# Latent x in four transfers with 16 grid columns outermost, and the first up-projection weights split during the output projection

## The chip, the cores and the metric

The kernel runs on one core of a Trainium2 chip, as one program. Its time is the device time of that core in microseconds (us), as the median of several runs. A profile of one execution goes with it. TensorE is called PE in the profile, ScalarE ACT, VectorE DVE, GpSimd POOL and SyncE SP; SyncE issues nearly all DMA transfers of this kernel.

## The reference

One layer of a hybrid diffusion backbone on two sets of tokens: 128 context tokens and 512 latent tokens, the latter on a grid of 8 rows and 64 columns, with 1024 channels each. All is float32. Both pass the same layer with their own modulation:

```python
def _layer(x, cond, attend, ...):
    sa, ca, ga, sf, cf, gf = _modulation(cond, w_mod, b_mod)
    h = _modulated_norm(x, norm_mix_g, sa, ca)
    p, q, k, v, gp, gn = _mixer_inputs(h, w_in, q_norm_g, k_norm_g)
    na = attend(q, k, v)
    pool = _pool_mixer(p, pool_w, pool_scale)
    x = x + ga * _merge(pool, na, gp, gn, w_pool_proj, w_na_proj, w_o)
    h = _modulated_norm(x, norm_ffn_g, sf, cf)
    x = x + gf * _conv_ffn(h, w_up, ffn_conv_w, ffn_conv_b, w_down)
    return x, k, v
```

`_modulated_norm` is an RMS norm over the channels, times (1 + scale), plus shift. Context tokens attend to each other. A latent token attends to the 128 cached keys and to a neighbourhood of 8 rows and 16 columns, with a bias for each head and relative position; the kernel takes queries in four blocks of 16 grid columns, each against a band of 32 columns. Pooling (windows of 2 to 16 tokens) and the width-3 convolution run along the token sequence in grid order, that is row after row.

## The kernel before

Every float32 product is made of three matmuls on a high and a low part: a weight tile `raw` is loaded by `load_raw`, and `split_to` makes `whi` (a cast on ScalarE, line 133) and `wlo` (a subtraction on VectorE, line 134). `load_w` does both. Tokens lie in five tiles of 128: tile 0 is the context, tiles 1 to 4 hold 16 grid columns of all 8 rows each, as two half-blocks of 8 columns (`hb`), each of them row after row.

The start, lines 302 to 337, is the stage that the first half of the change touches. The order of SyncE's issues is fixed: the small `vec`, two tiles `wm` of modulation weights, the context x (`in_xc`), latent tiles 1 and 2 into `vv`, the first value weights `wtok`, latent tiles 3 and 4 into `na` (both are borrowed memory), then further pairs `wm` and tiles `wtok` as the six buffers of `sp` come free. `load_x` issues two transfers a latent tile, one for each half-block, from `xl_blocks`, whose dimensions are half-block, row, column, channel. `normalise(t)` squares the tile on ScalarE (line 275), takes the root (277), scales on VectorE (280), transposes on TensorE (284) and copies the result to `xnT` (288, 290). `make_h` then makes `hhi` and `hlo`. `mod_rows` multiplies a pair `wm` with the conditioning on TensorE (149), and `tok_step` makes the value product (203 to 205), eight steps over the channels, in turn with those. Each DMA of SyncE marks its landing with one of eight semaphores taken in turn, and a later DMA with the same one waits for the earlier.

`to_grid_order` brings a result for all tokens from the order of the half-blocks into grid order; `blocks` is the view that it reads, `grid` the view that it writes. It is used in `gate_steps` for 16 gates (line 440, through `tanh_half`) and in `pool_group` for four pooling groups (434 to 437). `att_values` multiplies the attention's result by the inverse sums and writes it in grid order, 16 times for latent blocks (550). The bias table is laid out on the host by `_layout` in the same token order.

Later, the output projection runs in two halves of 512 channels: the first with `tok_step`, the second token tile by token tile in `out_product`, with the second norm's `second_h` in between. Then `up_a`, `up_w` and `up_b` make the up-projection. The first block's weights, `ra` and `rg`, are loaded and split behind that loop in the code, by lines 894 to 899. The order in which the engines get their instructions is not that of the code alone: a scheduler with a timeline of its own sets it when the program is built.

Of the kernel before, what the change touches and what calls it, by code (L numbers as in the profile page):

```python
# [11 lines left out]
F32R = mybir.dt.float32r  # L12
# [5 lines left out]
P = 128  # L18
# [6 lines left out]
ROWS = 8  # L25
# [3 lines left out]
NF = DFF // P  # L29
# [35 lines left out]
def body(ctx, tc, A):  # L65
    nc = tc.nc
    MULT, ADD, SUB, MIN = ALU.mult, ALU.add, ALU.subtract, ALU.min
# [6 lines left out]
    def pool(stack, name, bufs=1, side="left", space=bass.MemoryType.SB):  # L74
        return stack.enter_context(tc.tile_pool(name=name, bufs=bufs, space=space, reuse_waits="tile",
                                                side=side if space == bass.MemoryType.SB else None))
# [5 lines left out]
    wp = pool(ctx, "wp")  # L82
# [33 lines left out]
    def ps_small():  # L116
        return PS.tile([P, 512], F32, tag="sm", name="sm", bufs=8 - NACC)
# [6 lines left out]
    def load_raw(src, tp=None):  # L124
        r = (tp or wp).tile([P, 1024], F32, tag="raw", name="raw", bufs=SRAW if tp else 3)
        dma = nc.sync.dma_start(r, src)
        if tp or pinned[0] > 0:
            tc.keep_in_program_order(dma)
            pinned[0] -= 0 if tp else 1
        return r  # L130

    def split_to(raw, hi, lo):
        nc.scalar.copy(hi, raw)  # L133
        nc.vector.tensor_tensor(out=lo, in0=raw, in1=hi.bitcast(F32), op=SUB)  # L134
# [111 lines left out]
    xts = [VV[:, 2 * t:2 * t + 2, :].rearrange("p a b -> p (a b)") for t in range(3)]  # L246
    nas = na.rearrange("p a b -> p (a b)")
    xts += [nas[:, t * D:(t + 1) * D] for t in range(2)]

    xl_blocks = A["xl"].rearrange("(r hb c) d -> hb r c d", r=ROWS, c=8)  # L250
    junk = hlo.rearrange("p a b -> p (a b)")

    def load_x(t):
        if t == 0:
            nc.sync.dma_start(xts[0], A["xc"])
        else:
            for hb in range(2):
                nc.sync.dma_start(xts[t][hb * 64:hb * 64 + 64, :], xl_blocks[2 * (t - 1) + hb])

    def load_wv():  # L260
        wr.append(load_raw(A["wtok"][len(wr)], sp))
# [42 lines left out]
    for t in range(3):  # L304
        load_x(t)
    rows[0] = mod_scale_shift(0, rows[0])
    load_wv()
    for t in range(3, 5):
        load_x(t)
# [29 lines left out]
    for t in range(5):  # L339
        dst = VX if t == 0 else V[t - 1]  # L340
# [86 lines left out]
        return ap.rearrange("p (r hb c) -> p hb r c", r=ROWS, c=8)  # L427

    def blocks(ap):
        return ap.rearrange("p (hb r c) -> p hb r c", r=ROWS, c=8)  # L430

    def to_grid_order(fn, ctx_dst, lat_dst, ps):

        fn(ctx_dst, ps[0][:, :SEQ])
        d = grid(lat_dst)
        fn(d[:, 0:3], blocks(ps[0][:, SEQ:320]))
        fn(d[:, 3:8], blocks(ps[1][:, :320]))
# [97 lines left out]
    def att_values(pair, n, pts, rb):  # L535
        cs = CHUNKS[n]
        o = ps_small()
        for i, vt in enumerate(cs):
            for h in range(2):
                hd = (2 * pair + h) * DH  # L540
                nc.tensor.matmul(o[h * DH:(h + 1) * DH, :P], lhsT=vt[:, hd:hd + DH], rhs=pts[h][:, i * P:(i + 1) * P],  # L541
                                 start=(i == 0), stop=(i == len(cs) - 1))
        nc.tensor.transpose(o[:, P:2 * P], rb.rearrange("p a b -> p (a b)"), ident)
        r = at.tile([P, P], F32, name="rt", bufs=2)
        nc.scalar.copy(r, o[:, P:2 * P])
        if n == 4:
            nc.vector.tensor_tensor(out=na[:, pair, 0:SEQ], in0=o[:, :P], in1=r, op=MULT)
        else:
            dst = na[:, pair, SEQ:].rearrange("p (r n hb c) -> p n hb r c", r=ROWS, n=4, hb=2)[:, n]
            nc.vector.tensor_tensor(out=dst, in0=o[:, :P].rearrange("p (hb r c) -> p hb r c", hb=2, r=ROWS),  # L550
                                    in1=r.rearrange("p (hb r c) -> p hb r c", hb=2, r=ROWS), op=MULT)

    units = [(p, n) for p in range(4) for n in (4, 0, 1, 2, 3)]
    probs, pts = {}, {}
    for i in range(len(units) + 2):
        if i < len(units):
            probs[i] = att_scores(*units[i])
        next(mods, None)
        gate_fill(GF[0])
        if i - 1 in probs:  # L560
            pts[i - 1] = att_transpose(units[i - 1][1], *probs.pop(i - 1))
        gate_fill(GF[1])
        if i - 2 in pts:
            att_values(*units[i - 2], *pts.pop(i - 2))
        next(mods, None)
# [68 lines left out]
    for g in range(4):  # L634
        d = pool_group(g)
# [88 lines left out]
    for u in range(4):  # L724
        r = load_raw(A["wo"][4 + u])
# [76 lines left out]
    TI = {(4, HB): 0, (0, 0): 4, (0, HB): 8, (4, 0): 12}  # L802
    J = ((0, 64), (64, 192), (192, HB))

    xns = []
    for t in range(5):
        xns.append(out_product(t, lambda t: second_h(t, xns[t])))
# [8 lines left out]
    fw = pool(e6, "fw", 1, "right")  # L816
# [22 lines left out]
    def halves_of(w):  # L839
        return [tuple(x[:, i * 512:(i + 1) * 512] for x in w) for i in range(2)]  # L840
# [50 lines left out]
        nc.scalar.copy(ug[:, h1], pa[:, cs])  # L891


    ra, rg = load_raw(A["wup"][0]), load_raw(A["wup"][NF])
    w0 = []
    for tp_, r, e in ((wp, ra, ""), (fw, rg, "2")):
        hi, lo = [tp_.tile([P, 1024], F32R, tag=x + e, name=x + e, bufs=1 if e else 2) for x in ("whi", "wlo")]
        split_to(r, hi, lo)
        w0.append(halves_of((hi, lo)))

    def plain(x1_, x2_, n, c0):
        for (wa, wb), u in zip(w0, (us["a"][0], us["g"][0])):
# [133 lines left out]
def _layout(inp):  # L1036
# [30 lines left out]
    p, q, k, v, gp, gn = np.split(wi, np.cumsum([512, 512, 512, 512, 1024]), axis=1)  # L1067
# [14 lines left out]
    for g, w in enumerate(WINDOWS):  # L1082
        for c0, n in ((0, SEQ), (SEQ, LAT)):
            t = np.arange(n)
# [6 lines left out]
    r, c = np.arange(ROWS), np.arange(8)  # L1091
    idx = np.empty((4, P, 256), np.int64)
    for n in range(4):
        kb = min(max(16 * n - 8, 0), 32)
        qr = np.broadcast_to(r[None, :, None], (2, 8, 8)).reshape(-1)
        qc = (16 * n + 8 * np.arange(2)[:, None, None] + 0 * r[None, :, None] + c[None, None, :]).reshape(-1)
        kr = np.broadcast_to(r[None, :, None], (4, 8, 8)).reshape(-1)
        kc = (kb + 8 * np.arange(4)[:, None, None] + 0 * r[None, :, None] + c[None, None, :]).reshape(-1)
        ws = np.clip(qc - WIN_W // 2, 0, GRID_W - WIN_W)[:, None]
        ok = (kc[None] >= ws) & (kc[None] < ws + WIN_W)  # L1100
        dr = kr[None] - qr[:, None] + 7
        dc = np.clip(kc[None] - qc[:, None] + 15, 0, 30)
        idx[n] = np.where(ok, dr * 31 + dc, 15 * 31)
# [27 lines left out]
```

## Time and profile before

| what | us |
|---|---|
| median of 3 runs | 928.6 |
| lowest, highest | 926.58, 931.41 |
| profiled execution | 925.25 |
| its span, first to last instruction | 923.5 |
| TensorE busy in it | 873.9 (95%) |
| VectorE busy | 680.4 (74%) |
| ScalarE busy | 397.0 (43%) |
| GpSimd busy | 280.3 (30%) |

The profiled execution's own time is 1.75 us more than its span, for what lies around the first and the last instruction. The busy share is a mean over stages with different limits; where time can be won is read from the chain of work that ended last and from single stretches. "Releaser" is what ended an engine's idle time.

### The profile page before, as it was taken

Reading aid. Unit: us, or ns where it says so; the run is one execution under the profiler, and the core shown is the slowest. Engines: PE = TensorE matmul, PEld = TensorE weight load, DVE = VectorE, ACT = ScalarE, POOL = GpSimd, SP = SyncE. Lnnn points to the kernel's source line nnn. Section 1 sums busy time; section 2 is a strip of 40 time slices with the busy share of each in tenths; the row PEclk is TensorE's granted clock in tenths of the full one; section 3 lists DMA queues with packets and bytes.
Section 4 is the critical chain, followed back from the end, with each engine's and each line's share of the span. In section 5 each row is a group of like instructions: output and inputs, shape, how many; then the busy total and the mean of one; then the engine's idle time right before and its main releaser. Section 6 shows DMA issues by size and latency. Waiting matters only on the chain.

```text
span 923.5 us, 13399 instructions
## 1 busy us (share of the span) xinstructions
PE 873.9 (95%) x5234; PEld 783.5 (85%) x5234; DVE 680.4 (74%) x998; ACT 397.0 (43%) x712; POOL 280.3 (30%) x206
## 2 busy tenths in 40 slices
PE   3799999999998999999889899999999999999688
PEld 2578898887898999988689799999999999898677
DVE  3456986897479633535699888879788797887696
ACT  4351344445443422225766453635435354453340
POOL 2122000000000021322206434444334543339956
PEclk9999999999999999999989999999999999999989
DMA  8758425664365222264222421213222141222213
GB/s 235 248 206 270 153 75 171 200 227 137 104 197 159 73 84 73 70 233 155 92 69 103 137 78 59 92 61 122 70 69 92 46 136 51 89 92 80 92 45 115
DMA packets 33024, 112.20 MB, mean 121 GB/s; under 512 B 3857, under 2 KB 4529, under 8 KB 32705
## 3 DMA queue, kind: packets, MB, share of 16 engines
q1 hardware_dynamic: 31840, 107.91, 35.5%
q0 software_dynamic: 1120, 3.44, 1.3%
q8 instruction: 41, 0.67, 0.3%
q14 instruction: 23, 0.18, 0.1%
HBM read 104.50 MB, written 5.78 MB: 119 GB/s over the span
## 4 chain that ended last, share of the span: by engine, by line
PE 75%; DMA 8%; DVE 8%; POOL 4%; issue 3%; ACT 2%; SPq 0%; DVEq 0%; ACTq 0%; POOLq 0%
PE acc L836 22%; PE acc L219 20%; PE sm L989 4%; PE sm L990 4%; PE sm L991 4%; PE acc L203 3%; PE acc L205 3%; PE acc L204 3%; DVE wlo L134 2%; DMA na<-in_xl 2%; POOL acc L953 2%; DMA raw<-in_wo 2%; DVE cv L926 1%; DMA raw<-in_wup 1%; PE sm L541 1%
## 5 line engine op out<-in xcount | busy, mean ns | idle before, releaser
L133 ACT CAST whi<-raw 128x1024 fp32r<-128x1024 f32 (+1 forms) x86 | 81.2, 946 | 192.3 <-PE acc L836 73.6
L134 DVE TENSOR_TENSOR wlo<-raw,whi 128x1024 fp32r<-128x1024 f32 (+1 forms) x86 | 104.4, 1215 | 39.7 <-ACT whi L133 38.8
L836 PE MATMUL acc<-th,whi 128*128 128x322 f32 (+1 forms) x336 | 104.8, 316 | 7.0 <-ACT whi L133 4.3
L836 PE MATMUL acc<-th,wlo 128*128 128x322 f32 (+1 forms) x336 | 105.6, 315 | 1.3 <-DVE wlo L134 1.3
L836 PE MATMUL acc<-tl,whi 128*128 128x322 f32 (+1 forms) x336 | 105.4, 314 | 0.0
L219 PE MATMUL acc<-hhi,whi 128*128 128x320 f32 x320 | 91.7, 320 | 0.4 <-ACT t L440 0.4
L219 PE MATMUL acc<-hlo,whi 128*128 128x320 f32 x320 | 89.5, 313 | 0.0
L219 PE MATMUL acc<-hhi,wlo 128*128 128x320 f32 x320 | 88.6, 313 | 0.0
L858 POOL TENSOR_TENSOR ws<-raw 128x512 f32<-128x512 f32 x21 | 30.2, 1438 | 168.8 <-DVE wlo L134 104.3
L989 PE MATMUL sm<-dhi,ahi 128*128 128x512 f32 x190 | 72.6, 397 | 3.6 <-ACT dhi L133 1.7
L990 PE MATMUL sm<-dlo,ahi 128*128 128x512 f32 x190 | 75.1, 395 | 0.0
L836 PEld LDWEIGHTS acc<-th,whi 128*128 128x128 f32 x336 | 63.9, 191 | 10.3 <-ACT whi L133 5.8
L991 PE MATMUL sm<-dhi,alo 128*128 128x512 f32 x190 | 72.4, 395 | 0.0
L836 PEld LDWEIGHTS acc<-th,wlo 128*128 128x128 f32 x336 | 64.4, 192 | 3.1 <-DVE wlo L134 1.8
L836 PEld LDWEIGHTS acc<-tl,whi 128*128 128x128 f32 x336 | 64.3, 191 | 1.5
L133 ACT CAST whi<-ws 128x1024 fp32r<-128x1024 f32 x42 | 43.2, 1046 | 51.3 <-PE acc L836 41.0
L134 DVE TENSOR_TENSOR wlo<-ws,whi 128x1024 fp32r<-128x1024 f32 x42 | 53.6, 1292 | 13.3 <-ACT whi L133 13.3
L1001 DVE TENSOR_TENSOR acc<-sm,acc 128x512 f32<-128x512 f32 (+1 forms) x85 | 55.8, 676 | 9.2 <-PE sm L991 9.0
L836 PE MATMUL acc<-b1l,whi 128*128 128x322 f32 x184 | 57.8, 316 | 3.8 <-DVE b1l L134 3.8
L219 PEld LDWEIGHTS acc<-hhi,whi 128*128 128x128 f32 x320 | 58.2, 191 | 2.8 <-issue 1.3
L219 PEld LDWEIGHTS acc<-hlo,whi 128*128 128x128 f32 x320 | 58.2, 191 | 0.8 <-issue 0.7
L836 PE MATMUL acc<-b1h,whi 128*128 128x322 f32 x184 | 57.5, 316 | 0.8 <-ACT b1h L133 0.8
(322 smaller groups left out, 2313.6 us busy)
## 6 DMA issues: line engine op xcount, KB each, us to landing
raw<-in_wup SPq DMA_DIRECT2D x44, 512.0 KB, 4.6
mw<-in_wmT SPq DMA_DIRECT2D x32, 512.0 KB, 4.6
raw<-in_wdn SPq DMA_DIRECT2D x22, 512.0 KB, 3.4
raw<-in_wmt SPq DMA_DIRECT2D x20, 512.0 KB, 3.5
raw<-in_wm SPq DMA_DIRECT2D x16, 512.0 KB, 9.3
raw<-in_wtok SPq DMA_DIRECT2D x12, 512.0 KB, 11.6
bias<-in_bias SPq DMA_DIRECT2D x16, 384.0 KB, 4.7
raw<-in_wab SPq DMA_DIRECT2D x8, 512.0 KB
```

The costliest lines, as they stand in the source:

```text
L133: nc.scalar.copy(hi, raw)
L134: nc.vector.tensor_tensor(out=lo, in0=raw, in1=hi.bitcast(F32), op=SUB)
L203: nc.tensor.matmul(ps[t], lhsT=xh, rhs=wh, start=(kt == 0), stop=False)
L204: nc.tensor.matmul(ps[t], lhsT=xh, rhs=wl, start=False, stop=False)
L205: nc.tensor.matmul(ps[t], lhsT=xl, rhs=wh, start=False, stop=(kt == KT - 1))
L219: nc.tensor.matmul(o[:, :n], lhsT=w[:, k], rhs=cut(x, k, c, n), start=st and a, stop=sp and b)
L836: upped[0] = nc.tensor.matmul(ps[:, cs], lhsT=a[:, c], rhs=b[:, k, cs], start=start and first, stop=last, skip_group_check=skip and not st ...
L858: nc.gpsimd.tensor_tensor(out=s[:, 1], in0=a21, in1=a22, op=ADD)
L989: nc.tensor.matmul(ps, lhsT=xh, rhs=hi[:, sl], start=(j == 0), stop=False)
L990: nc.tensor.matmul(ps, lhsT=xh, rhs=lo[:, sl], start=False, stop=False)
L991: nc.tensor.matmul(ps, lhsT=xl, rhs=hi[:, sl], start=False, stop=(j == GRP - 1))
L1001: nc.vector.tensor_tensor(out=o, in0=ps, in1=o, op=ADD)
```

## The change

Latent x comes in one transfer a tile, four in all, with the 16 columns of the tile as the outermost dimension, then the 8 rows. Inside a half-block the tokens so stand column after column and no longer row after row; `blocks`, the multiplication of `att_values` and the host's bias indices follow. And the first block's up-projection weights are loaded ahead of the loop over `out_product`, one of the two split there.

```diff
-    xl_blocks = A["xl"].rearrange("(r hb c) d -> hb r c d", r=ROWS, c=8)
+    xl_blocks = A["xl"].rearrange("(r t c) d -> t c r d", r=ROWS, c=16)
...
         else:
-            for hb in range(2):
-                nc.sync.dma_start(xts[t][hb * 64:hb * 64 + 64, :], xl_blocks[2 * (t - 1) + hb])
+            nc.sync.dma_start(xts[t], xl_blocks[t - 1])
...
     def blocks(ap):
-        return ap.rearrange("p (hb r c) -> p hb r c", r=ROWS, c=8)
+        return ap.rearrange("p (hb c r) -> p hb r c", r=ROWS, c=8)
...
-            nc.vector.tensor_tensor(out=dst, in0=o[:, :P].rearrange("p (hb r c) -> p hb r c", hb=2, r=ROWS),
-                                    in1=r.rearrange("p (hb r c) -> p hb r c", hb=2, r=ROWS), op=MULT)
+            nc.vector.tensor_tensor(out=dst, in0=blocks(o[:, :P]), in1=blocks(r), op=MULT)
...
+    w0a, rg = load_w(A["wup"][0]), load_raw(A["wup"][NF])
     xns = []
     for t in range(5):
         xns.append(out_product(t, lambda t: second_h(t, xns[t])))
...
-    ra, rg = load_raw(A["wup"][0]), load_raw(A["wup"][NF])
-    w0 = []
-    for tp_, r, e in ((wp, ra, ""), (fw, rg, "2")):
-        hi, lo = [tp_.tile([P, 1024], F32R, tag=x + e, name=x + e, bufs=1 if e else 2) for x in ("whi", "wlo")]
-        split_to(r, hi, lo)
-        w0.append(halves_of((hi, lo)))
+    hi, lo = [fw.tile([P, 1024], F32R, tag=x, name=x, bufs=1) for x in ("whi2", "wlo2")]
+    split_to(rg, hi, lo)
+    w0 = [halves_of(w0a), halves_of((hi, lo))]
```

In `_layout` the four index lines of the bias (queries `qr`, `qc`, keys `kr`, `kc`) swap the places of row and column in the same way.

What the built program makes of it on SyncE, at its first transfers: before, from the context x on, with the semaphores that each waits for:

```order
L255 DMA vv<-in_xc 128x1024
L258 DMA vv<-in_xl 64x1x1024 x4
L126 DMA raw<-in_wtok 128x1024 [waits DMAHW0_49]
L258 DMA na<-in_xl 64x1x1024 [waits DMAHW1_49]
L258 DMA na<-in_xl 64x1x1024 [waits DMAHW2_49]
L258 DMA na<-in_xl 64x1x1024 [waits DMAHW3_49]
L258 DMA na<-in_xl 64x1x1024 [waits DMAHW4_49]
L126 DMA raw<-in_wm 128x1024 [waits DMAHW5_49]
L126 DMA raw<-in_wm 128x1024 [waits DMAHW6_49]
L126 DMA raw<-in_wm 128x1024 [waits DMAHW7_49]
```

And with the change, the same place, to the same second pair of `wm`:

```order
L256 DMA vv<-in_xc 128x1024
L258 DMA vv<-in_xl 128x1x1024 x2
L126 DMA raw<-in_wtok 128x1024
L258 DMA na<-in_xl 128x1x1024
L258 DMA na<-in_xl 128x1x1024 [waits DMAHW0_49]
L126 DMA raw<-in_wm 128x1024 [waits DMAHW1_49]
L126 DMA raw<-in_wm 128x1024 [waits DMAHW2_49]
L126 DMA raw<-in_wm 128x1024 [waits DMAHW3_49]
```

Half of the x transfers are gone, and with them most of the waits ahead of the second `wm` pair: the eight semaphores go round later, so that the last x transfer waits for the first one (`vec`), where before the fifth to eighth waited for the `wm` pair, the context x and the first half of latent tile 1.

On ScalarE, at the output projection: the last `mhi`, the casts of that projection's weights (`whi` and `w1h`), the first two casts for the up-projection (the last `whi` row), and the squares of the residual. Before:

```order
L133 CAST whi<-raw 128x1024
L666 ACTIVATE mhi<-t_613 128x640
L133 CAST w1h<-raw 128x1024
L133 CAST whi<-raw 128x1024 x2
L133 CAST w1h<-raw 128x1024 x3
L133 CAST whi<-raw 128x1024 x2
L717 ACTIVATE o_t,sq_4051<-x_4042 128x512 x5
```

With the change:

```order
L133 CAST whi<-raw 128x1024
L665 ACTIVATE mhi<-t_609 128x640
L133 CAST w1h<-raw 128x1024
L133 CAST whi<-raw 128x1024 x2
L133 CAST w1h<-raw 128x1024 x3
L133 CAST whi<-raw 128x1024 x2
L716 ACTIVATE o_t,sq_4047<-x_4038 128x512 x5
```

Nothing moved here but the numbers of lines and buffers: the up-projection's first cast stood ahead of the squares already. The same holds for the other engines: TensorE, VectorE, ScalarE and GpSimd run the same rows in the same order before and after.

## Rows read from the trace of the kernel before

**Rows 1.** The page of the whole span: the chain that ended last.

```profile
PE 75%; DMA 8%; DVE 8%; POOL 4%; issue 3%; ACT 2%; SPq 0%; DVEq 0%; ACTq 0%; POOLq 0%
PE acc L836 22%; PE acc L219 20%; PE sm L989 4%; PE sm L990 4%; PE sm L991 4%; PE acc L203 3%; PE acc L205 3%; PE acc L204 3%; DVE wlo L134 2%; DMA na<-in_xl 2%; POOL acc L953 2%; DMA raw<-in_wo 2%; DVE cv L926 1%; DMA raw<-in_wup 1%; PE sm L541 1%
```

**Rows 2.** The chain in order of time, 0 to 80: start, us, what.

```profile
2.60 9.11 DMA vv<-in_xl
...
11.72 16.92 DMA na<-in_xl
...
31.62 1.57 PE sm L284 x8
33.19 1.86 PE sm L149 x16
```

**Rows 3.** Windows: length, busy time by engine, granted clock, DMA share, GB/s.

```profile
0.00:8.00 8.00, 1.95 (x16) 0.43 (x16) 0.50 (x3) 3.29 (x6) 1.99 (x9) 1.00 0.76 254
6.00:8.00 2.00, 1.27 (x12) 0.20 (x8) 0.00 (x0) 0.00 (x0) 0.00 (x0) 1.00 1.03 393
9.84:28.72 18.88, 8.65 (x31) 6.82 (x32) 8.10 (x16) 7.76 (x16) 2.84 (x2) 1.00 0.90 224
12.00:14.00 2.00, 1.55 (x8) 1.57 (x8) 0.30 (x1) 0.59 (x1) 0.00 (x0) 1.00 0.51 164
14.00:20.00 6.00, 2.35 (x10) 1.57 (x8) 2.08 (x6) 3.14 (x8) 0.00 (x0) 1.00 0.95 253
24.00:26.00 2.00, 0.08 (x1) 0.09 (x1) 0.10 (x1) 2.00 (x5) 0.00 (x0) 1.00 1.05 199
32.00:36.00 4.00, 4.00 (x26) 2.09 (x25) 2.00 (x6) 1.56 (x4) 0.00 (x0) 0.57 0.52 177
36.00:72.00 36.00, 36.00 (x237) 26.68 (x236) 20.51 (x39) 15.32 (x22) 7.17 (x3) 1.00 0.64 224
```

**Rows 4.** DMA issues of the whole span: operation, count, KB each, us to landing.

```profile
raw<-in_wm SPq DMA_DIRECT2D x16, 512.0 KB, 9.3
...
vv<-in_xl SPq DMA_DIRECT2D x4, 256.0 KB
na<-in_xl SPq DMA_DIRECT2D x4, 256.0 KB
...
vv<-in_xc SPq DMA_DIRECT2D x1, 512.0 KB
...
vv<-in_cv POOLq DMA_DIRECT2D x1, 256.0 KB, 6.8
...
vec<-in_vec SPq DMA_DIRECT2D x1, 131.0 KB, 2.1
```

**Rows 5.** SyncE's issues in order of time, 0 to 40: start, us.

```profile
2.60 2.71 SPq L258 DMA_DIRECT2D vv<-in_xl  x4
...
5.83 6.48 SPq L258 DMA_DIRECT2D na<-in_xl  x4
13.34 6.44 SPq L126 DMA_DIRECT2D raw<-in_wm  x4
```

**Rows 6.** ScalarE in order of time: the first and the last Square of x.

```profile
9.84 1.06 ACT L275 ACTIVATE hlo<-vv 128x1024 fp32r<-128x1024 f32 x1 [1.19 <-DMA vv<-in_xc]
...
28.72 1.06 ACT L275 ACTIVATE hlo<-na 128x1024 fp32r<-128x1024 f32 x1 [2.66 <-DMA na<-in_xl]
```

**Rows 7.** Groups by shape, whole span: busy us, mean ns, idle before.

```profile
L440 ACT ACTIVATE t<-acc 128x320 f32<-128x320 f32 x16 | 7.0, 440 | 0.0
...
L550 DVE TENSOR_TENSOR na<-sm,rt 128x128 f32<-128x128 f32 x16 | 4.5, 282 | 0.9 <-ACT rt L545 0.9
...
L440 ACT ACTIVATE t<-acc 128x128 f32<-128x128 f32 x16 | 4.4, 274 | 0.0
```

**Rows 8.** Waits of TensorE, 120 to 400: us in total, times, longest.

```profile
PE acc L219 <- ACT t L440: 0.4, 1, 0.4
```

**Rows 9.** ScalarE in order of time, 416 to 430: first up-projection cast.

```profile
423.17 1.05 ACT L133 CAST whi<-raw 128x1024 fp32r<-128x1024 f32 x1 [2.38 <-DMA raw<-in_wup]
```

More of the change, by code (lines that the diff above doesn't have):

```diff
@@ L1094, in _layout @@
         kb = min(max(16 * n - 8, 0), 32)
[L1095 to L1098, printed above, removed]
+        qr = np.broadcast_to(r[None, None, :], (2, 8, 8)).reshape(-1)
+        qc = (16 * n + 8 * np.arange(2)[:, None, None] + c[None, :, None] + 0 * r[None, None, :]).reshape(-1)
+        kr = np.broadcast_to(r[None, None, :], (4, 8, 8)).reshape(-1)
+        kc = (kb + 8 * np.arange(4)[:, None, None] + c[None, :, None] + 0 * r[None, None, :]).reshape(-1)
         ws = np.clip(qc - WIN_W // 2, 0, GRID_W - WIN_W)[:, None]
```

## The prediction

> **What bounds the kernel now.** I read the chain that ended last first, because only time on it can be won. Over the whole span 75% of it is TensorE and 8% are DMAs, and one item of that 8% stands out by name: the transfers of the latent x into the tiles na, 2% [rows 1]. The chain in order of time shows where they lie: from 2.60 to 28.64 us it consists of x transfers alone, 9.11 us into the tiles vv and 16.92 into na; then come the last tile's transposes at 31.62 and, at 33.19, the product with the second pair of modulation weights, after which the chain stays on TensorE [rows 2]. From 36 to 72 us TensorE is busy 36.00 of 36.00 us while the DMA engines are busy 0.64 of the time [rows 3]. So the start waits for x, and what follows is a train of matmuls that is not starved: if it leaves earlier, everything behind it moves.
>
> Why x is slow is in the windows. Its eight transfers are of 256 KB and go to 64 partitions each, beside transfers of 512 KB to 128 [rows 4]. At 12 to 14 us the DMA share is 0.51 at 164 GB/s, against 1.03 and 393 GB/s at 6 to 8 us [rows 3]: about half of the 16 DMA engines work. The outermost dimension of an x transfer's source is 8 (grid rows); that a transfer is dealt out over as many engines as this count is my inference from the half share. At 32 to 36 us the share is again 0.52, when x has long landed, which I read as the same eight engines working off the weights that queued behind x. SyncE is held up too: the four issues into na take 6.48 us and the next four 6.44, where the four into vv take 2.71 [rows 5].
>
> **The change part by part.** *The x loads.* Eight transfers become four of twice the size, with the same bytes, on 128 partitions and with an outermost count of 16. The order of SyncE's instructions shows the issues: before, each of the last four x transfers waits for an earlier transfer's semaphore (there are eight, taken in turn); after, only the very last waits, for the small vec load of the start. So x is issued by about 6 us, and the weights behind it follow sooner.
>
> When has the last x tile landed? Ahead of it and with it stand vec (131 KB), two modulation tiles and one value-weight tile, the context x and four x tiles (eight of 512 KB), and the cached values (256 KB) [rows 4]: 4483 KB, 4.59 MB. By 8 us 254 GB/s x 8 us = 2.03 MB have gone [rows 3], so 2.56 MB are left. From the bytes to the consumer's start there is a lag: the context x ends at 131 + 3 x 512 + 256 KB = 1.97 MB, that is at about 8 us, and its Square starts at 9.84 [rows 6]: 1.8 us. The rate isn't known, because no row shows this pattern. Its upper end is 393 GB/s (all engines on contiguous loads): 6.5 us, data at 16.3. The lower is 199 GB/s at 24 to 26 us, when the engines were as busy (1.05) but slow, with x among the traffic: 12.9 us, data at 22.7. Nearest are the same rows on half the engines, 164 x 2 = 328, and x mixed with weights as it will be, 253 at 14 to 20 us [rows 3]. I take the middle, 290: 2.56 / 0.290 = 8.8 us, data at 8 + 8.8 + 1.8 = 18.6.
>
> The last tile's Square starts at 28.72 now [rows 6]. It can't come before the work ahead of it: between 9.84 and 28.72 ScalarE is busy 7.76 us and VectorE 8.10 [rows 3], so not before 9.84 + 8.10 = 17.9 even with no wait between them. ScalarE's order is unchanged: the Square of tile 4 stands behind the root of tile 3, and that behind a cast that waits for VectorE, so some waiting stays. I take 19.7, 1.8 after that bound and 1.1 after the data. Gain 28.72 - 19.7 = 9.0 us; at the fast end 28.72 - 17.9 = 10.8; with data at 22.7 it is 6.0.
>
> What is late next? The pair of modulation weights right behind x in the queue: 1024 KB, 1.05 MB more, 3.61 in all. TensorE reads them at 33.19, 4.5 us after that Square [rows 2, 6], so they are needed at 24.2. At 290 GB/s they are there at 8 + 12.4 + 1.8 = 22.2, in time; at 199 at 27.9, and the gain is then 33.19 - 27.9 = 5.3. Behind that the loads come as buffers fall free, as before, and the share of 0.64 leaves room. TensorE's clock is the other uncertainty: the granted clock is 0.57 of full from 32 to 36 us, right behind the wait for x [rows 3]. The new start will have such a stretch too; 3 us more or less of half clock are 1.5 us either way.
>
> *The order inside a half-block.* Tokens now stand by column, then row, so blocks() reads PSUM and the tile rt in steps of 8 elements where it read straight on. It concerns 16 gates and 4 pooling groups on ScalarE and 16 multiplications on VectorE. I cost them at nothing: a straight read with a stepped write (320 elements, 440 ns) is no dearer than the straight copy next to it, 274 ns for 128, with 0.86 ns for each element more [rows 7]; no row shows a stepped read. What hides a little more is TensorE's lead over ScalarE: it waited for these gates once, 0.4 us [rows 8]. The other end of the bound is that every such element takes twice its time: 512 x 0.86 = 0.44 us, 20 times 8.8, and 16 x 0.28 = 4.5 on VectorE [rows 7]; 13.3 us if all of it lay on the path.
>
> [...]
>
> *The up-projection weights.* In the order of the built program nothing moves: the cast of these weights stands behind the output projection's own casts before and after, and it already runs at 423.17, during that projection [rows 9]. The split of the second tile is left where it was. So 0 us: nothing is moved that would need a cover, and there is no gain either.
>
> **Sum.** The profiled execution takes 925.25 us for its span of 923.5. Forecast 925.25 - 9.0 = 916.2. The median of the runs shown is 928.6, 3.35 above the profiled one, and the prediction is for such a median: 928.6 - 9.0 = 919.6.
>
> **The rivals.** *x stays slow* (same side, smaller). The rows of x that one engine fetches are still 256 KB apart in memory. For it: at 24 to 26 us a share of 1.05 brought only 199 GB/s, so something other than the number of engines is slow while x is fetched. Against: 253 GB/s at 14 to 20 us with the same rows in flight. Gain 5.3, or 923.3; at 170 GB/s, little above what half the engines gave, the weights are there at 31.0 and the gain is 2.2, or 926.4.
>
> [...]
>
> *Hidden anyway* (no change). The weight pair becomes the last arrival. For it: it stands behind x in the same queue, and TensorE waits for it next. Against: at 290 GB/s it is 2 us early, and to eat the whole gain it would have to come at 33.19, a rate of 3.61 / 23.4 = 154 GB/s, less than even half the engines gave. Time 926 to 929.
>
> *Stepped reads* (the other side). The gates and the multiplications take longer, and TensorE waits at the accumulators for them. It decides from 9.0 us of loss on; the 13.3 bounded above leave 4.3 over, a time of 932.9 at the most. Against: all of it would have to lie on the path, where one wait of 0.4 us shows now.
>
> *The change does nothing.* For the weights this is my forecast; for x the built program does show four transfers to 128 partitions.
>
> **How the numbers follow.** Half a percent, 4.6 us, is about what a measurement of this kernel can tell from no change: the three runs lie 4.8 apart. Forecast, gain 7 to 10: 0.60. More, up to the 10.8 of the fast end and the clock's 1.5: 0.08. x stays slow, gain 2 to 7: 0.20, two thirds of it above 4.6. Hidden: 0.07. Stepped reads: 0.05, of which 0.03 slower by more than 0.5% where other losses join. That makes faster 0.60 + 0.08 + 0.13 = 0.81, slower 0.03, and the same 0.16. The range goes from the fast end with the clock's 1.5 us and the spread of a median of such runs, 0.8, 928.6 - 13.1 = 915.5, to the lower part of the slow rival, a gain of 2.6: 926.
>
> **What would show it.** The last Square on x at 19 to 20.5 us in place of 28.72; SyncE's four x issues done by 6 us; a DMA share near 1 until about 22 us with no stretch at 0.5; the second weight pair's product at about 24 and the same full TensorE behind it; the gates still at 440 ns and the multiplications at 282; the casts of the up-projection weights 9 us earlier, like all their neighbours. If the Square comes at 20 and the span falls by less than 5, the train was starved later; if the first 20 us stay under 200 GB/s, x stayed slow.

## The result, and the profile after

The median is 918.94 us (four runs, 917.25 to 920.83); the kernel before, timed in turn with it on the same chip, has 927.59 (four runs, 926.05 to 931.41). The ratio is 0.9894, 95% interval 0.9869 to 0.992: faster, by 8.65 us, where 9.0 were forecast. The profiled execution took 920.83 us, its span is 919.1.

The chain that ended last, from the page of the changed kernel, answers to [rows 1] (line numbers have moved by one or two in places: L836 is L837 now, L989 to L991 are L987 to L989):

```profile
PE 77%; DVE 8%; POOL 4%; DMA 4%; issue 3%; ACT 2%; SPq 0%; DVEq 0%; ACTq 0%; POOLq 0%
```

DMA has gone from 8% to 4%. The same chain in order of time, 0 to 80 us (start, us, what), answers to [rows 2]:

```profile
4.83 14.42 DMA na<-in_xl
19.27 1.15 ACT hlo L275 x2
20.41 0.47 ACT xnT L290
20.89 0.31 ACT hhi L299
21.24 1.22 PE acc L203 x2
...
24.17 1.92 PE sm L284 x16
26.09 1.00 PE sm L149 x16
27.09 0.43 PE acc L203
```

Of x transfers 14.42 us are left where [rows 2] have 9.11 and 16.92. They end at 19.27 in place of 28.72, and behind them stands no transfer, only ScalarE and TensorE at work: the last tile's transposes and the product with the second pair of modulation weights (26.09 in place of 33.19) follow one another. The tile is another one, too: the chain of before ended x with the fourth latent tile, this one with the third, whose Square is the one at 19.27.

The windows of the changed kernel, columns as in [rows 3]:

```profile
0.00:8.00 8.00, 1.82 (x16) 0.43 (x16) 0.50 (x3) 3.29 (x6) 1.99 (x9) 1.00 0.73 250
6.00:8.00 2.00, 1.44 (x16) 0.20 (x8) 0.00 (x0) 0.00 (x0) 0.00 (x0) 1.00 1.02 401
12.00:14.00 2.00, 0.77 (x4) 0.80 (x5) 1.00 (x3) 1.54 (x4) 0.00 (x0) 1.00 1.05 248
14.00:20.00 6.00, 4.89 (x22) 3.91 (x20) 5.17 (x8) 3.60 (x6) 2.11 (x1) 1.00 1.04 245
22.00:24.00 2.00, 2.00 (x7) 1.42 (x6) 1.21 (x3) 1.24 (x4) 0.00 (x0) 1.00 1.01 401
32.00:36.00 4.00, 4.00 (x23) 2.68 (x23) 3.17 (x5) 0.94 (x3) 2.39 (x1) 1.00 0.84 314
36.00:72.00 36.00, 36.00 (x212) 27.84 (x211) 21.12 (x38) 13.36 (x19) 9.47 (x11) 1.00 0.67 229
```

No stretch stands at half a share any more: the 0.51 at 12 to 14 us is 1.05. But while x is in flight all sixteen engines bring only about 245 GB/s, and 401 before and behind it. TensorE is full from 36 to 72 us as before.

SyncE's issues in order of time (start, us) answer to [rows 5], and ScalarE's squares (start, us, idle time before in brackets) to [rows 6]:

```profile
2.60 1.36 SPq L258 DMA_DIRECT2D vv<-in_xl  x2
...
4.83 1.24 SPq L258 DMA_DIRECT2D na<-in_xl  x2
6.11 6.68 SPq L126 DMA_DIRECT2D raw<-in_wm  x4
```

```profile
10.63 1.06 ACT L275 ACTIVATE hlo<-vv 128x1024 fp32r<-128x1024 f32 x1 [1.85 <-DMA vv<-in_xc]
...
19.27 1.06 ACT L275 ACTIVATE hlo<-na 128x1024 fp32r<-128x1024 f32 x1 [1.46 <-DMA na<-in_xl]
...
21.42 1.06 ACT L275 ACTIVATE hlo<-na 128x1024 fp32r<-128x1024 f32 x1
```

The last Square stands at 21.42, 7.3 us earlier, and shows no idle time in front of it. Two things end there together: ScalarE's work ahead of it (the copy at 20.32, a cast, the root from 21.09 to 21.38) and the landing of the fourth latent tile, issued at 5.41 and there 16.0 us later, at 21.40. The issues at work between 6 and 7.5 us (KB each, us to landing; the two of `wm` are the second pair, landed at 22.4 and 23.7):

```profile
raw<-in_wm SPq DMA_DIRECT2D x2, 512.0 KB, 16.4
na<-in_xl SPq DMA_DIRECT2D x1, 512.0 KB, 16.0
```

The groups by shape and the first cast for the up-projection answer to [rows 7, 9]:

```profile
L440 ACT ACTIVATE t<-acc 128x320 f32<-128x320 f32 x16 | 7.0, 440 | 0.0
L550 DVE TENSOR_TENSOR na<-sm,rt 128x128 f32<-128x128 f32 x16 | 6.2, 384 | 0.9 <-ACT rt L545 0.9
```

```profile
416.50 1.05 ACT L133 CAST whi<-raw 128x1024 fp32r<-128x1024 f32 x1 [2.27 <-DMA raw<-in_wup]
```

The gates cost what they did; the multiplications take 384 ns and no longer 282.

**Where the time came from, and where some went back.** I follow the starts of the same matmuls in both traces. The first value product behind the second weight pair starts at 27.02 (34.98 before), 7.96 us earlier; from 36 us on the lead is 8.3. It stays so to 187 us of before, is 6.3 at 190.8 (184.54 now), 5.0 at 280, 6.6 at 285, 5.8 at 480, 4.7 at 860 and still 4.7 at the end.

Part of this is TensorE's clock, whose granted value is 1.00 or 0.50 of full speed in both traces (0.50 from 182 to 184 us here, and from 33 to 35 before). From 181.1 on it is at half for 3.4 us where before has none; half of 3.4 us is 1.7 of the 2.0 us there. At 281 it is the other way round (before has 3.4 us of it), and the lead grows again by 1.5. Around 454 to 464 it is at half for 10.2 us, before for 6.8, and the lead shrinks by 0.9. A window of each trace over the first of these places, before and after (the clock is the third number from the end):

```profile
170.00:200.00 30.00, 29.61 (x228) 25.20 (x228) 26.43 (x68) 14.89 (x45) 0.00 (x0) 1.00 0.62 200
```

```profile
170.00:200.00 30.00, 29.11 (x204) 24.29 (x203) 26.83 (x68) 11.98 (x37) 0.00 (x0) 0.94 0.65 210
```

The rest is not the clock's. At 280 TensorE waits 3.5 us for a cast on ScalarE (`pdh`) where before it waits 2.3 (us in total, times, longest; before, then after):

```profile
PE acc L219 <- ACT pdh L133: 2.3, 1, 2.3
```

```profile
PE acc L219 <- ACT pdh L133: 3.5, 1, 3.5
```

In the profiles below this wait is 2.2 to 3.6, and 3.6 in the one with the weights alone, so it does not go with the loads of x. And between 500 and 860 another 1.2 us goes in small steps at full clock in both, which I have not traced further. The prediction's reading of a small gain in the span, "the train was starved later", is then true of a part, and the clock took another. The profiled pair, 4.4 us of span apart, understates the change for another reason too: 925.25 was a quick execution of the kernel before, whose runs went from 924.87 to 936.46 in one series of 19, and 920.83 is the slowest of the four runs of the changed one. The moment the kernel before has its x varies. In the profile shown the last Square is at 28.72; in two kernels below that load x with the same kind of transfers it is at 31.78 and 30.37.

### The profile page after: what moved, and what is told of

Its sections match the earlier page's. It is cut to its first block, busy times and chain, and to the rows that moved or that the text cites. A ratio compares the mean times of both kernels' runs of the same rounds, so it can differ in the third digit from the quotient of the medians.

```text
span 919.1 us, 13388 instructions
## 1 busy us (share of the span) xinstructions
PE 874.8 (95%) x5234; PEld 784.5 (85%) x5234; DVE 682.1 (74%) x998; ACT 397.1 (43%) x712; POOL 281.5 (31%) x206
## 4 chain that ended last, share of the span: by engine, by line
PE 77%; DVE 8%; POOL 4%; DMA 4%; issue 3%; ACT 2%; SPq 0%; DVEq 0%; ACTq 0%; POOLq 0%
PE acc L219 21%; PE acc L837 20%; PE acc L203 4%; PE sm L987 4%; PE sm L988 4%; PE acc L205 4%; PE sm L989 4%; PE acc L204 4%; DVE wlo L134 3%; POOL acc L951 2%; DVE cv L924 2%; DMA raw<-in_wdn 2%; DMA na<-in_xl 2%; ACT whi L133 1%; PE sm L541 1%
## 5 line engine op out<-in xcount | busy, mean ns | idle before, releaser
L837 PE MATMUL acc<-th,whi 128*128 128x322 f32 (+1 forms) x336 | 105.6, 318 | 6.9 <-ACT whi L133 3.9
L837 PE MATMUL acc<-th,wlo 128*128 128x322 f32 (+1 forms) x336 | 106.2, 317 | 1.2 <-DVE wlo L134 1.2
L837 PE MATMUL acc<-tl,whi 128*128 128x322 f32 (+1 forms) x336 | 106.2, 316 | 0.0
L987 PE MATMUL sm<-dhi,ahi 128*128 128x512 f32 x190 | 72.7, 398 | 3.8 <-ACT dhi L133 1.8
L837 PEld LDWEIGHTS acc<-th,whi 128*128 128x128 f32 x336 | 64.5, 193 | 10.9 <-ACT whi L133 6.0
L989 PE MATMUL sm<-dhi,alo 128*128 128x512 f32 x190 | 72.4, 395 | 0.0
L837 PEld LDWEIGHTS acc<-th,wlo 128*128 128x128 f32 x336 | 64.9, 193 | 3.0 <-DVE wlo L134 1.7
L837 PEld LDWEIGHTS acc<-tl,whi 128*128 128x128 f32 x336 | 64.8, 193 | 1.4
L837 PE MATMUL acc<-b1l,whi 128*128 128x322 f32 x184 | 58.2, 318 | 3.8 <-DVE b1l L134 3.8
L837 PE MATMUL acc<-b1h,whi 128*128 128x322 f32 x184 | 57.8, 318 | 0.9 <-ACT b1h L133 0.9
```

The source lines that it names most:

```text
L837: upped[0] = nc.tensor.matmul(ps[:, cs], lhsT=a[:, c], rhs=b[:, k, cs], start=start and first, stop=last, skip_group_check=skip and not st ...
L987: nc.tensor.matmul(ps, lhsT=xh, rhs=hi[:, sl], start=(j == 0), stop=False)
L989: nc.tensor.matmul(ps, lhsT=xl, rhs=hi[:, sl], start=False, stop=(j == GRP - 1))
```

## The experiments

Each was timed in turn with the kernel before on one chip. "Last Square" and GB/s are from the one profiled execution; the kernel before and the changed one stand first.

| kernel | median us | ratio to before, 95% | last Square at | GB/s 10 to 14 |
|---|---|---|---|---|
| before | 927.6 to 930.3 | 1 | 28.72 | 164 |
| changed | 918.94 | 0.9894 (0.9869 to 0.992) | 21.42 | 254 |
| 1 weights only | 926.87 | 0.9971 (0.9938 to 1.0003) | 31.78 | 137 |
| 2 rows outermost | 928.93 | 0.9988 (0.9961 to 1.0015) | 31.48 | 180 |
| 3 channel halves | 919.18 | 0.988 (0.9827 to 0.9933) | 20.21 | 282 |
| 4 host order | 917.73 | 0.9861 (0.9814 to 0.9909) | 18.06 | 406 |
| 5 padded pitch | 920.01 | 0.9904 (0.9868 to 0.9941) | 21.79 | 250 |
| 6 small gap | 922.22 | 0.9927 (0.9899 to 0.9956) | 21.46 | 272 |
| 7 fast x, straight reads | 915.6 | 0.986 (0.9832 to 0.9887) | 18.74 | 377 |
| 8 x only | 919.97 | 0.9902 (0.9873 to 0.9931) | 21.02 | 270 |
| 9 quarter pieces | 923.14 | 0.9936 (0.9908 to 0.9963) | 25.24 | 236 |
| 10 order only | 931.57 | 1.0012 (0.9987 to 1.0037) | 30.37 | 152 |
| 11 stepped write | 920.59 | 0.9894 (0.9868 to 0.992) | 21.22 | 255 |

My theory was that the number of engines that carry x sets when the train of matmuls leaves; the rivals were that the fewer transfers and waits on SyncE do it, that the weights do, and that the stepped reads take something back. When the rate came out at 245 and not 290, a second question was added: what keeps x slow on sixteen engines.

**1. The weights alone.** The kernel before with the second part of the change.

```diff
+    w0a, rg = load_w(A["wup"][0]), load_raw(A["wup"][NF])
     xns = []
...
-    ra, rg = load_raw(A["wup"][0]), load_raw(A["wup"][NF])
...
```

> The kernel before with the second half of the change alone: the up-projection weights loaded ahead of the out_product loop, x still in eight transfers. My theory (the scheduler had already put that cast there, so this half is worth nothing): the same time as before within 0.3%, the last Square of x near 28.7 us, the first up-projection cast near 423 us. The rival (the two halves share the gain): 2 us or more of the 8.65 us come with this half.

The interval holds 1: nothing that can be measured, though by itself it leaves room for up to 0.6%. x lands late in this profile (31.78), so the span is not to be compared with that of before.

**8. x alone.** The changed kernel with that part taken back.

> The changed kernel without the edit on the up-projection weights: their load and split stand behind the loop over the token tiles again, as in the kernel before. The first half of the change is all of the gain: the time of the changed kernel, 918.9, within 0.3%, the last Square on x at 21.4 and the shift at the first dense matmuls 8.0 us. If the weights had brought a part of it (the run with them alone was at 0.9971, with an interval that ends at 1.0003), it is 921 to 922.

919.97 and a last Square at 21.02: within the intervals, some 3 us either way, the whole gain is the first half's. The lead at the first value product is 7.3 us, not 8.0, with 6.8 us of half clock ahead of it (from 19.5 on) that the changed kernel lacks.

**2. Eight outermost.** The changed loads with the rows outermost; the token order of the rest is left as it is and no longer fits, so this one serves for timing alone.

```diff
-    xl_blocks = A["xl"].rearrange("(r t c) d -> t c r d", r=ROWS, c=16)
+    xl_blocks = A["xl"].rearrange("(r t c) d -> t r c d", r=ROWS, c=16)
```

> The changed kernel with one thing undone: each of the four x transfers to 128 partitions has the 8 grid rows outermost and the 16 columns inside. Tokens then stand in another order than the rest of the program takes for granted, so attention and pooling work on the wrong neighbours; all sizes and the order of instructions stay. My theory (the outermost count sets how many DMA engines work): a DMA share near 0.5 again between 10 and 16 us, the last Square of x at 27 to 29 us, 6 to 9 us slower than the changed kernel. The rival (four fewer transfers and the SyncE waits that go with them were the gain): the last Square stays near 21.4 us and the time near 919.

A window of this kernel's trace:

```profile
10.00:14.00 4.00, 1.01 (x5) 1.04 (x6) 0.92 (x2) 1.44 (x3) 0.53 (x1) 1.00 1.03 180
```

The whole gain is gone, with four transfers of 128 partitions and SyncE done with x by 6.1 us. Here the outermost count decides, 8 or 16, not the number of transfers. The half share that I expected at 10 to 16 us did not show (1.03), and yet I take eight engines to carry x. The semaphore records kept in the traces say so: a transfer's semaphore rises in steps while it lands, sixteen for the context x in every kernel, eight for each transfer of latent x in the kernel before and in 1, 2, 9 and 10 (and one more step at the issue), sixteen in the changed kernel and the others. I read a step as one engine that is done, since the share is 0.51 in windows with x in eight steps (before at 12 to 14 us, 9 at 16 to 18). The other eight engines, by the same reading, are at the weights queued behind x: in 2 a tile `wm` issued at 10.37 has eight of its steps by 21.0 us and the other eight only from 34.6 on; in the kernel before the first tile `wm` behind x has eight between 16.8 and 18.0 us and eight between 28.3 and 30.2. But 2 does not halve the engines alone: the rate for each busy engine falls too, to 180 / 16 / 1.03 = 11 GB/s, from 254 / 16 / 1.04 = 15 in the changed kernel.

**3. Eight transfers, sixteen outermost.** Each x transfer cut in two by channels, so that SyncE waits as before.

```diff
-            nc.sync.dma_start(xts[t], xl_blocks[t - 1])
+            for h in range(2):
+                hs = slice(h * 512, (h + 1) * 512)
+                nc.sync.dma_start(xts[t][:, hs], xl_blocks[t - 1][:, :, hs])
```

> The changed kernel with each x transfer cut into two by channels, 512 each: eight transfers again, with the same four waits on SyncE as before the change, but 16 columns outermost and 128 partitions. My theory (engines, not waits): the last Square of x within 1.5 us of the changed kernel's 21.42, the time within 2 us of 919. The rival (the waits were the gain): SyncE's last x issue at about 11.7 us as before, the last Square at 26 us or later, 5 us or more slower.

SyncE's issues into `na` end at 11.12 (12.31 before) and the time is that of the changed kernel: the waits on SyncE were not the gain.

**4. x in one piece.** A second copy of latent x, laid out on the host in the order of the tiles, so that a transfer reads 512 KB straight on.

```diff
+    a["xb"] = a["xl"].reshape(ROWS, 4, 16, D).transpose(1, 2, 0, 3).reshape(LAT, D)
...
-    xl_blocks = A["xl"].rearrange("(r t c) d -> t c r d", r=ROWS, c=16)
+    xl_blocks = A["xb"].rearrange("(t p) d -> t p d", p=P)
```

> The changed kernel with a second copy of latent x as an input, laid out on the host in the order of the tiles, so that each of the four transfers reads 512 KB in one piece. Theory that rows 256 KB apart in memory keep x slow (248 GB/s at 12 to 18 us in the changed kernel with all 16 engines busy): the rate between 8 and 18 us rises to 340 GB/s or more, x tiles 3 and 4 are there 3 us earlier, ScalarE's order then sets the last Square at about 19.5, gain 1 to 2 us more. The rival (memory is not it, the mixture with the other traffic is): 220 to 270 GB/s again and the same Square at 21.4.

```profile
10.00:14.00 4.00, 2.12 (x9) 1.75 (x10) 2.78 (x7) 3.38 (x9) 0.30 (x1) 1.00 1.04 406
14.00:20.00 6.00, 5.09 (x27) 4.47 (x28) 5.26 (x10) 4.81 (x11) 2.86 (x2) 1.00 1.03 378
```

The same engines, 406 GB/s. The last tile has landed at 16.21 and its Square is at 18.06, behind a cast that waits 1.05 us for VectorE: once x is fast, the engines' own order sets it, as the prediction's bound of 17.9 has it. That the numbers are so near is in part chance, since here the first Square stands at 8.69 and not at 9.84. The train of matmuls leaves 12.2 us earlier than before (at 68.6 us of before); 3.6 of that are given back by 192 us, where 6.8 us run at half clock (177.0 on). After this run I held the distance of 256 KB between the rows of a column for the cause of the slow x.

**5 and 6. The distance, and the pieces.** Both from copies on the host, with transfers otherwise as in the changed kernel. In 5 every grid row is one column longer, so that the rows of a column are 260 KB apart; in 6 x lies in tile order, but with 4 KB free behind every eight rows, so that a transfer can't be joined into one piece.

```diff
-    xl_blocks = A["xl"].rearrange("(r t c) d -> t c r d", r=ROWS, c=16)
+    xl_blocks = A["xb"][:, 0:64].rearrange("r (t c) d -> t c r d", c=16)
...
+    a["xb"] = np.zeros((ROWS, 65, D), np.float32)
+    a["xb"][:, :64] = a["xl"].reshape(ROWS, 64, D)
```

```diff
-    xl_blocks = A["xl"].rearrange("(r t c) d -> t c r d", r=ROWS, c=16)
+    xl_blocks = A["xb"][:, :, 0:8]
...
+    a["xb"] = np.zeros((4, 16, 9, D), np.float32)
+    a["xb"][:, :, :8] = a["xl"].reshape(ROWS, 4, 16, D).transpose(1, 2, 0, 3)
```

> The changed kernel, with latent x read from a copy laid out on the host in which each grid row has 65 columns in place of 64, so that the eight rows of a column are 260 KB apart and no longer 256 KB. Transfers, their shape, their order and all that follows are those of the changed kernel. Theory one, the distance: rows that lie a power of two apart fall on the same part of memory and wait for each other; then 8 to 14 us run at 380 to 410 GB/s, the last Square on x stands at about 18, the second weight pair's product at about 22, and the time is that with the contiguous copy, 917.7 (1 to 2 us under the changed kernel). Theory two, the scatter: any source that isn't read in one piece is slow; then 230 to 260 GB/s and the last Square at 21.4 as in the changed kernel, 918.9.

> The changed kernel, with latent x read from a copy on the host in the order of the tiles, but with 4 KB left free behind every column's eight rows, so that the source of a transfer is 16 pieces of 32 KB and not one piece of 512 KB. Theory one (the distance between rows is what makes the loads slow): 390 to 410 GB/s at 8 to 14 us and the last Square at about 18, as with the contiguous copy; 917.7. Theory two (any source that is not in one piece is slow): 230 to 260 GB/s, last Square at 21.4, 918.9.

Windows of 5, then of 6:

```profile
10.00:14.00 4.00, 0.80 (x4) 0.83 (x5) 1.32 (x5) 2.89 (x6) 0.53 (x1) 1.00 1.04 250
14.00:20.00 6.00, 3.95 (x22) 2.98 (x20) 4.99 (x7) 3.35 (x6) 1.91 (x1) 1.00 1.04 238
```

```profile
10.00:14.00 4.00, 1.26 (x6) 1.29 (x7) 1.22 (x4) 2.89 (x6) 0.00 (x0) 1.00 1.03 272
14.00:20.00 6.00, 4.40 (x20) 3.38 (x18) 4.03 (x8) 3.60 (x6) 1.77 (x1) 1.00 1.04 240
```

The distance falls as a cause: neither another distance nor almost straight reading helps. Against experiment 4 the only thing that 6 changes is that a transfer can't be read as one run of 128 rows; the same bytes, on sixteen engines in both, then come at 240 to 272 and not at 378 to 406. So I take it to be how the transfer is divided, not where x lies in memory. (6 is slower in time than the changed kernel with the same landing; its profile has half clock at 22, 210 and 275 us, 3.4 each; whether that is the reason is open.)

**9. Pieces to 32 partitions.** Transfers of 32 partitions, of 8 pieces of 4 rows, again with gaps so that nothing is joined: is a transfer in pieces slow there too?

```diff
-    xl_blocks = A["xl"].rearrange("(r t c) d -> t c r d", r=ROWS, c=16)
+    xl_blocks = A["xb"][:, :, :, 0:4]
...
-            nc.sync.dma_start(xts[t], xl_blocks[t - 1])
+            for q in range(4):
+                nc.sync.dma_start(xts[t][32 * q:32 * q + 32, :], xl_blocks[t - 1, q])
...
+    a["xb"] = np.zeros((4, 4, 8, 5, D), np.float32)
...
```

> The changed kernel with each latent tile of x in four transfers of 32 partitions, every one of 8 pieces of 4 rows, from a copy laid out on the host that keeps the token order and leaves a row free behind every 4, so that the pieces can't be joined. Half the engines carry x then, as before the change. [...] Theory two (a transfer in several pieces costs its packets more, wherever they go): packets still 200 ns and more, x at 160 GB/s or less on eight engines, the last Square at 24 to 30, and 922 to 927.

A window in which x comes alone, and SyncE's issues:

```profile
16.00:18.00 2.00, 1.88 (x8) 1.48 (x8) 0.12 (x1) 1.60 (x4) 0.00 (x0) 1.00 0.51 205
```

```profile
2.60 7.59 SPq L259 DMA_DIRECT2D vv<-in_xb  x8
...
11.42 6.85 SPq L259 DMA_DIRECT2D na<-in_xb  x8
```

The rate goes against theory two. At the same share of 0.51 the engines bring 205 GB/s, where before they brought 164 [rows 3]: 25% more from the same number of engines, and per engine (205 / 16 / 0.51 = 25 GB/s) what contiguous loads give in experiment 4 (406 / 16 / 1.04 = 24). So a transfer in pieces is not slow as such. The Square and the time are those of theory two all the same: beside the weights the total is 236 (10 to 14 us), and with sixteen issues SyncE sends the last of x only by 18.3 us, so that the last Square comes at 25.24 and the time is 923.14, against 21.42 and 918.94 in the changed kernel. The pieces to 32 partitions come fast where they run alone, and the late issues cost more than that gives.

**10 and 11. The token order.** 10 is the kernel before with the order, the stepped reads and the bias indices of the changed one; 11 is the changed kernel with the multiplications read straight and written in steps.

```diff
-    xl_blocks = A["xl"].rearrange("(r hb c) d -> hb r c d", r=ROWS, c=8)
+    xl_blocks = A["xl"].rearrange("(r hb c) d -> hb c r d", r=ROWS, c=8)
...
```

```diff
-            dst = na[:, pair, SEQ:].rearrange("p (r n hb c) -> p n hb r c", r=ROWS, n=4, hb=2)[:, n]
-            nc.vector.tensor_tensor(out=dst, in0=blocks(o[:, :P]), in1=blocks(r), op=MULT)
+            dst = na[:, pair, SEQ:].rearrange("p (r n c) -> p n c r", r=ROWS, n=4)[:, n]
+            nc.vector.tensor_tensor(out=dst, in0=o[:, :P].rearrange("p (c r) -> p c r", r=ROWS),
+                                    in1=r.rearrange("p (c r) -> p c r", r=ROWS), op=MULT)
```

> The kernel before with the token order of the changed one (column after column inside a half-block, stepped reads, bias indices) and eight transfers by half-block as before, 8 columns outermost in place of 8 rows. Theory one: the order costs its 1.6 us on VectorE (16 multiplications at 384 ns in place of 282) and what TensorE loses in attention, so 0.5 to 2 us over the kernel before, ratio 1.0005 to 1.002, with a half clock between 170 and 200 us as in the changed kernel. Theory two: VectorE's time is hidden and the half clock there comes by chance; then the multiplications are at 384 ns, the shift of the matmuls against the kernel before doesn't move between 150 and 280 us, and the ratio is 1.000. In both the last Square on x stands near 28.7.

> The changed kernel with the multiplications of att_values read straight on and written in steps (in0 and in1 in the order of the tokens, the output view with the row innermost), the same result. If stepped reads are what VectorE pays for, they go from 384 ns to 282 or near it; if a step on either side is, they stay near 384 or go over it, the output's steps being 256 bytes. In time: if the multiplications are hidden, 918.9 as the changed kernel; if they were on the path, 1.6 us less, 917.3. The shift against the kernel before then holds at 8 us between 36 and 280 us, without a half clock near 181.

The multiplications of 10, then of 11, in the groups by shape:

```profile
L550 DVE TENSOR_TENSOR na<-sm,rt 128x128 f32<-128x128 f32 x16 | 6.2, 385 | 0.9 <-ACT rt L545 0.9
```

```profile
L550 DVE TENSOR_TENSOR na<-sm,rt 128x128 f32<-128x128 f32 x16 | 6.1, 379 | 0.9 <-ACT rt L545 0.9
```

A step on either side costs VectorE the same 0.1 us (385 and 379 ns, against 282). In time the order costs nothing that can be measured (1.0012, interval from 0.9987), and in 10 the lag of the matmuls behind those of before is 0.1 us or less from 36 to 277 us, with no half clock in between: theory two. (At 280 it is 0.8, the wait for `pdh` of 3.2 us in place of 2.3.) A half clock at 181 us shows in 11, with straight reads, so it does not come of the stepped reads; and 10 has the order without it.

**7. Fast x in the old order.** Straight reads and x in four contiguous transfers, from a copy on the host.

```diff
-    xl_blocks = A["xl"].rearrange("(r hb c) d -> hb r c d", r=ROWS, c=8)
+    xl_blocks = A["xb"].rearrange("(t p) d -> t p d", p=P)
...
+    a["xb"] = a["xl"].reshape(ROWS, 8, 8, D).transpose(1, 0, 2, 3).reshape(LAT, D)
```

> The token order, blocks, the multiplications and the bias indices of the kernel before (row after row inside a half-block, so straight reads), the weights of the changed kernel, and x read from a copy laid out on the host in that order, in four contiguous transfers of 128 partitions. It differs from the run with the contiguous copy in column order by the stepped reads alone. Theory one, the stepped reads cost more than their own time: the 16 multiplications are at 282 ns in place of 384, no half clock shows between 170 and 200 us, the shift of about 12 us at the first dense matmuls is still over 10 us at 280 us, and the time is 914 to 916. Theory two, the earlier start gives part of itself back whatever the reads are (loads of weights that come late, or the clock): a half clock shows between 170 and 200 us here too, the shift falls to 8 to 9 us there, and the time is 917 to 918.

By its profile it is theory one: no half clock between 170 and 200 us, a lead of 11.6 us at 73 us and at 285. But 10 and 11 take the explanation away, and against 4 the times don't differ (0.986 and 0.9861). It has the lowest median of all; its interval still touches that of the changed kernel.

## Why the prediction was right

The time, 919.6 forecast and 918.94 measured, and the sign come from the named cause: an outermost count of sixteen, with which sixteen engines carry x (experiments 2, 3 and 8), while the weights bring nothing that shows (1 and 8). That the sizes agree so well is in part luck. Term by term:

- **The rate.** I took 290 GB/s between 393 and 199. It was 245 to 254, in size the other near row named, 253, but not for the reason given there, "x mixed with weights": between 10.6 us, where the context x has landed, and 12.3, where the first engine is done with the second latent tile, hardly anything but x comes (a copy of 128 KB beside it), and still at 255 (the window below). Twice the engines bring 1.6 times the 164 of before. The 328 of 164 x 2 did not come either. The last tile has landed at 21.40, not at 18.6, and the 1.1 us that I allowed behind the data for ScalarE's order were not needed, so that its Square is at 21.42 and not 19.7. With the profiled landing of before, 28.72, that is a gain of 7.3 at this point.

```profile
10.60:12.30 1.70, 0.00 (x0) 0.00 (x0) 0.16 (x1) 1.44 (x3) 0.53 (x1) 1.00 1.02 255
```

- **What it is subtracted from.** The forecast of 9.0 came close because a second number was off the other way: 28.72 is early for the kernel before (31.78 and 30.37 in the two other profiles with its kind of transfers, a mean of 30.3 with it). The profiles of the changed kernel, 8 and 11, with the same loads, have 21.02 to 21.42, and 5, with the longer row, 21.79: a mean of 21.4, 8.9 earlier. These are single profiles, three and four of them; as far as they go, both errors cancel, and that they do so nearly is luck.
- **Everything behind it moves.** The sum carried the gain at the start whole to the end, but for 1.5 us of clock either way. In the profiled pair a lead of 8.3 us at 36 ends as 4.7, in 4 one of 12.2 as 7.5, in 7 one of 11.6 as 9.4. The sum had nothing for what the train gives back, and the medians are 8.65 apart all the same, the two profiled executions lying at opposite ends of their runs. How much an average execution gives back stays open.
- **What is late next.** The second weight pair was the feared arrival. It has landed at 23.7, in time for the 24.2 that the forecast needed. Its product starts at 26.02, 1.8 us later than that, nearly all of it the Square's 1.7, and TensorE is at work without a pause from 21.24 to there: its last wait is for ScalarE's cast `hhi`, which stands behind the third tile's Square in ScalarE's order. So in this profile the third tile's landing sets the start of the train, and the fourth's no longer does. From 14 to 36 us the longest waits of TensorE (us in total, times, longest) name ScalarE and VectorE, and no transfer is among its waits:

```profile
PE acc L203 <- ACT hhi L299: 1.8, 1, 1.8
PE sm L284 <- DVE vv L280: 0.6, 1, 0.6
```

- **x stays slow**, a rival at 0.20, was right that something besides the number of engines slows x, and wrong in its price: I worked it at 199 and 170 GB/s. Its cause as I put it, rows 256 KB apart, is refuted by 5 and 6.
- **The stepped reads.** Costed at nothing: right on ScalarE (440 ns, as before), wrong on VectorE, where 282 ns are 384, 1.6 us over 16. It is hidden (10), so the sum doesn't move. The step of 32 bytes has a price on one engine, the 0.1 us a multiplication, and none on the other.
- **The weights.** 0 forecast, nothing measurable (1 and 8). Their first cast moved by 6.7 us and not 9, like its neighbours: the lead of all matmuls there is 6.6.
- **The clock.** I looked for the half clock right behind the start. In the changed kernel's profile none is there; it lies at 181 and, longer, at 454. In 5 and 8 it lies at 20 us, for 6.8 us, and 181 shows none; 3 and 6 have 3.4 us of it at 20 and 22. The 1.5 us that I allowed either way is the price of one such stretch of 3.4 us.

**Why x is slow on sixteen engines** is shown as far as this: it goes with how the transfer is divided over the engines and partitions (4 against 6, 9 against before), and neither the distance of the rows (5) nor gaps between near pieces (6 against 9, which has gaps too) explain it. A busy engine brings 164 / 16 / 0.51 = 20 GB/s before, 15 in the changed kernel, 11 in 2, 24 in 4 and 25 in 9.

What in the division does it, no run here shows: not why an engine brings 20 GB/s before and 15 in the changed kernel, nor why one brings less in 9 beside the weights, 236 / 16 / 0.85 = 17 GB/s at 10 to 14 us, than the 25 without them.

The origin of the half clock between 177 and 191 us stays open too: it shows in the changed kernel and in 2, 3, 4 and 11, in 6 at 210, and not in before, 1, 5, 7, 8, 9 and 10; none of the order, the reads and an early start sorts these by itself.

## What to carry to other kernels

Read how a transfer is divided before its bytes: in these kernels the outermost count went with the number of engines at work (8 against 16 was 8 to 9 us), and x that can be read in runs of 128 rows came at 406 GB/s (10 to 14 us), x in 16 pieces on the same engines at 250 to 272, with the rows of a column 256 or 260 KB apart as with gaps of 4 KB. A shorter start is worth what the train behind it keeps: follow the lead of the same matmul to the end, and check in other profiles of the same loads whether the landing you subtract from is a typical one.

## What was not expected of the hardware

- Sixteen pieces of 32 KB with 4 KB between them come at 240 to 272 GB/s, the same rows without the gaps at 378 to 406.
- A multiplication of 128x128 on VectorE takes 282 ns when the last run of reads and writes is 8 elements long, and 379 to 385 with steps of 32 bytes in the reads or of 256 in the write; ScalarE's reads of PSUM in the same steps cost nothing (440 ns for 320).
- The last Square on x, which follows the landing at once, differs by 3 us between three profiles with 64-partition transfers (28.72, 30.37, 31.78), while in five with whole tiles to 128 partitions in 16 pieces it stays within 0.8 (21.02 to 21.79). Each is one execution of another program; whether the program or the execution makes the difference is open.
- Twice the engines brought x at 1.6 times the rate and not at twice it (164 GB/s at 12 to 14 us before, 255 at 10.6 to 12.3 in the changed kernel).
